# Tile 3's logits and ranks ahead of the first expert's row products, and one weight piece split on other engines

## The chip, the cores and the metric

The kernel runs on one core of a Trainium2 chip. A core has the matrix engine TensorE (PE; its weight loads are listed apart as PEld), VectorE (DVE), ScalarE (ACT), GpSimd (POOL) and SyncE (SP), and 16 DMA engines that they feed through queues. Each engine works through its own instructions in order and waits on semaphores for the others. The metric is the time of one launch in microseconds on the device; each time is one run or the median of several.

## The reference

Two layers, each a token mixer (attention, mLSTM and a state-space branch) followed by a mixture of experts, over 512 tokens of 1024 features. What the change touches lies between the output projection and the first experts:

```python
mix = jnp.einsum('bsc,cd->bsd', heads, w_out[l])
x = _layernorm(DEEPNORM_ALPHA * x + mix, ln1_g[l], ln1_b[l])
...
glog = jnp.einsum('bsd,dg->bsg', x, wg) + bg                 # 4 groups
gp, gi = lax.top_k(jax.nn.softmax(glog, -1), 1)              # the best group
elog = jnp.einsum('bsd,gde->bsge', x, we) + be               # 4 experts in each
elog = jnp.einsum('bsge,bsg->bse', elog, one_hot(gi[..., 0]))
ep, ei = lax.top_k(jax.nn.softmax(elog, -1), 2)              # the best two of it
ep = ep / jnp.sum(ep, -1, keepdims=True)
combine = jnp.sum(one_hot(gi * 4 + ei, 16) * (gp * ep)[..., None], axis=2)
h = jax.nn.silu(einsum(x, w_gate)) * einsum(x, w_up)         # for each of 16 experts
h = h * combine[..., None]
return jnp.einsum('bsef,efd->bsd', h, w_down)
```

So each token goes to two of 16 experts. The kernel computes an expert only for the tokens that chose it, in blocks of 96 rows.

## The kernel before

Tokens stand in four tiles of 128. Float32 products are made of three passes over operands that are split into a high part (a copy on ScalarE) and a low part (a subtraction, on VectorE unless another engine is named). One helper, `split`, does this; its line is L409. Most other instructions go through a second helper that records them, and so have line 229 whatever issued them. A weight piece is 128x1024; an expert has six: four for its two first products (up and gate) and two for the last (down).

The stage in question runs once in each layer, around 320 to 370 us in layer 0 and 530 us later in layer 1. For each tile it makes the second half of the output projection, adds it to the residual, normalizes it, and computes the 20 router logits of the tile from transposed rows. From the logits it ranks groups and experts with comparisons (`low` is a constant mask that breaks ties), which gives `al`, a tile's one-hot of chosen experts. Matmuls of `al` with a triangle of ones (`strict`) and with ones (`onesb`) count each token's place within its expert's block; `key` is that place, and `ohf` (expert 0) and `ohs` (the others) are one-hots of `key` against 0 to 95. Expert 0's rows are not gathered but made on TensorE, as products of each tile with `ohf`. Every other expert gets an index: matmuls of `ohs` with a table of row numbers, then VectorE's `slr` and `slx`. GpSimd then gathers the rows by that index from `x1d`, a copy of the normalized tiles in DRAM (L1445), TensorE transposes them and VectorE and ScalarE split them.

The order in which this stage is written out is the string `WSEQ`, one step a word, with a tile's number behind most letters. A framework then assigns instructions to engines by this order and by when it expects operands, so that neighbouring steps may change places on an engine.

- `S` splits a piece of expert 0; `A` issues weight loads for the coming experts as far as buffers are free (`ahead`, L276 in the queue).
- `m` is a tile's projection; `e` adds it to the residual, transposes the tile's half on TensorE and has ScalarE copy it out of PSUM; `b` and `r` are mean, variance and reciprocal root; `g` and `f` normalize, one half of the columns on ScalarE and GpSimd (L1791 and L1799), the other on VectorE, and `f` ends with the store to `x1d` (L1802); `k` stores the tile to `acc` as well (L1806).
- `l` multiplies the transposed tile with the router's weights `wrg`; `c` finishes its logits `lg`; `Kab` ranks tiles a to b-1 and makes their one-hots.
- `Z` is expert 0's row product of one tile; `H` makes expert 1's index and gathers its rows.

The transposed halves of two tiles share one buffer of the pool from which weight loads get theirs. Stores and loads alike stand in SyncE's queue, in the order of the text, so a load that waits for a buffer holds back the store behind it. Expert 0's first three pieces are split in `S0` to `S2`; the rest of those below `PX` right behind the stage, with GpSimd doing the subtraction, in buffers that the projection has given back:

```python
for n in range(PRE, PX):          # PRE = 3, PX = 4
    ex[0].split(n, G, True)
```

A piece that has not been split by then is split when its product is written out, by ScalarE and VectorE.

Of the kernel before, what the change touches and what calls it, by code (L numbers as in the profile page):

```python
# [61 lines left out]
RES3 = 8  # L62
PROG = 1
SPARE = 0
PX = 4
RES2 = 12
LP = 30
NPA = 3
# [15 lines left out]
HOLD = 8  # L84
HK = 0
HE = 0
WSEQ = 'S0 S1 S2 A m0 e0 b0 r0 r0 r0 r0 g0 A m1 e1 b1 r1 r1 r1 r1 g1 l0 c0 f0 k0 A m2 l1 c1 K02 e2 b2 r2 r2 r2 r2 g2 f1 k1 A m3 Z0 Z1 l2 c2 f2 k2 e3 b3 r3 r3 g3 r3 r3 f3 K23 Z2 l3 c3 K34 H Z3'
WPIN = ''
NU = 7
WOG = (0, 2)  # L90
# [121 lines left out]
def tile_trunk(ctx: ExitStack, tc: tile.TileContext, ins, out, dbg=None, depth=DEPTH):  # L212
# [22 lines left out]
    V, A, G, T = Pinned(nc.vector, "V"), Pinned(nc.scalar, "A"), nc.gpsimd, Pinned(nc.tensor, "T")  # L235
# [20 lines left out]
    def small(shape, dt=F32, tag="s", bufs=1):  # L256
        return sm.tile(shape, dt, name=nm(tag), tag=tag, bufs=bufs)
# [162 lines left out]
    def mm3(p, ah, al, bh, bl, start=True, stop=True):  # L420
        T.matmul(p, ah, bh, start=start, stop=False)
        T.matmul(p, ah, bl, start=False, stop=False)
        T.matmul(p, al, bh, start=False, stop=stop)
# [134 lines left out]
    for l in range(depth):  # L558
# [1054 lines left out]
        def ahead(keep, upto=6 * E):  # L1613

            while todo and len(pool.whole) > keep and pool.spare(SPARE if keep == RES0 else 3) and 6 * todo[0][0].e + todo[0][1] < upto:
                m, n = todo.pop(0)
                if n not in m.raw:
                    m.load(n)
# [8 lines left out]
        order = (3, 2, 0, 1)  # L1627
# [28 lines left out]
        def wo_mm(p, i, q, w, first, last):  # L1656
            s = slice(i * 128, (i + 1) * 128)
            for a in range(2):
                j = 2 * q + a
                cc = slice(a * 512, a * 512 + 512)  # L1660
                mm3(p.ap, xh[j][:, s], xl[j][:, s], w[0][:, cc], w[1][:, cc],
                    start=(first and a == 0), stop=(last and a == 1))
# [34 lines left out]
        wo = []  # L1697
# [5 lines left out]
        def lend(q):  # L1703
            pool.whole += [NS + 2 * q, NS + 2 * q + 1]
# [15 lines left out]
        def route(a, b):  # L1720

            n = b - a
            ranks(a, b)


            dv = df.rearrange("p (i g) e -> p i g e", i=NT)
            V.tensor_tensor(oa[:, a:b], dv[:, a:b, 1:5], thr4[:, None, None, 1].to_broadcast([128, n, 4, 4]), op=OP.is_lt)
            V.tensor_tensor(oh1[:, a:b].rearrange("p i g e -> p (i g) e"), df[:, a * 5:b * 5],
                            thr4[:, None, 0].to_broadcast([128, n * 5, 4]), op=OP.is_lt)
            V.tensor_tensor(al[:, a:b].rearrange("p i (g e) -> p i g e", g=4), oa[:, a:b], bc(oh1[:, a:b, 0]), op=OP.mult)  # L1730
            if not prk:
                prk.append(P5.get(NT * E))
            p = prk[0]
            v = p.v("p (i e) -> p i e", i=NT)
            if a == 0:
                T.matmul(p[:, 0:b * E], strict, al[:, 0:b].rearrange("p i e -> p (i e)"), start=True, stop=False,
                         skip_group_check=True)
            for i in range(a):
                T.matmul(v[:, a:b], onesb, al[:, i, None, :].to_broadcast([128, n, E]), start=(i == 0), stop=False,
                         skip_group_check=True)  # L1740
            for i in range(a, b - 1):
                T.matmul(v[:, i + 1:b], onesb, al[:, i, None, :].to_broadcast([128, b - 1 - i, E]),
                         start=False, stop=False, skip_group_check=True)
            if a:
                T.matmul(p[:, a * E:b * E], strict, al[:, a:b].rearrange("p i e -> p (i e)"), start=False, stop=True,
                         skip_group_check=True)
            r = V.scalar_tensor_tensor(key[:, a:b], v[:, a:b], 1.0, al[:, a:b], op0=OP.add, op1=OP.mult)
            for e in range(2):
                ex[e].hot(key[:, :, e], a, b)
            return r  # L1750

        class Tile_:
# [1 line left out]
                self.i, self.z, self.s = i, xr[i], slice(i * 128, (i + 1) * 128)  # L1754
                self.ph = PHS[i]

            def mm(self):
                p = self.p = ps[self.i] if PROG else P4.get()
                for a, q in list(enumerate(order))[PROG:]:
                    wo_mm(p, self.i, q, wo[a], a == 0, a == 3)  # L1760

            def evac(self):
                self.ev = evac(self.p, self.i, 1)
# [46 lines left out]
        def mark():  # L1810
            return tc.keep_in_program_order(G.memset(small([128, 1], tag="mark", bufs=2), 0.0))

        tiles = [Tile_(i) for i in range(NT)]
        kins, mk = None, []
        for c in WSEQ.split():
            if c[0] == "Z":
                i = int(c[1])
                ex[0].xz(i, tiles[i].z)
                if i < NT - 1:
                    tiles[i].z.free()  # L1820
                continue
            if c[0] == "K":
                pin[0] = WPIN
                kins = route(int(c[1]), int(c[2]))
                pin[0] = False
                continue
            if c == "H":
                ex[1].go()
                mk += [None, mark()]
                continue  # L1830
            if c == "A":
                ahead(RES0)
                continue
            if c[0] == "S":
                pin[0] = WPIN
                ex[0].split(int(c[1]), lent=True)
                pin[0] = False
                continue
            t = tiles[int(c[1])]
            pin[0] = WPIN  # L1840
            {"m": t.mm, "e": t.evac, "b": t.bn, "r": t.r, "l": t.logits, "c": t.lgs, "g": t.g, "f": t.f, "k": t.keep}[c[0]]()
            pin[0] = False
        free(*wo[PROG:])
        free(lgt, prk, ln1)
# [1 line left out]
        for q in order[PROG:]:  # L1846
            lend(q)
        for n in range(PRE, PX):
            ex[0].split(n, G, True)
# [4 lines left out]
        for _ in range(NU):  # L1854
            m, n = todo.pop(0)
# [10 lines left out]
        m1, m2 = small([128, NT, 5], tag="m1"), small([128, NT, 4], tag="m2")  # L1866
# [116 lines left out]
        with tc.If(rv > 0), tc.For_i(0, rv, 1):  # L1983
# [43 lines left out]
            m = Expert(load_gu, load_dn)  # L2027
# [120 lines left out]
        for i in range(NT):  # L2148
            n = norms[i]
# [79 lines left out]
```

## Time and profile before

| | |
|---|---|
| median of 3 runs | 1076.05 us (1075.78 to 1082.33) |
| profiled execution | 1076.42 us, of which the span is 1074.7 us |
| mean granted clock of TensorE | 0.971 of full |
| busy share of the span | TensorE 93%, VectorE 78%, ScalarE 60%, GpSimd 25% |

The profile is one execution. Times below are us from the start of its span. A group's last bracket on a timeline tells for how long the engine had stood idle and which operation, of which engine, ended that. A granted clock of 1.00 is TensorE's full 2.4 GHz, 0.50 its 1.2 GHz.

### The profile page before, as it was taken

How to read it: one execution, taken by the hardware profiler on the slowest of the kernel's cores; microseconds unless marked ns; L12 is line 12 of the kernel's file. 1: busy time of each engine (PE TensorE's matmuls, PEld its weight loads, DVE VectorE, ACT ScalarE, POOL GpSimd, SP SyncE). 2: the span in 40 equal slices, each digit the busy share in tenths (PEclk: the TensorE clock that was granted, in tenths of full speed). 3: DMA queues.
4: the chain of work that ended last, by engine and by line, in shares of the span. 5: the costliest groups of instructions: out<-in, count | busy, mean ns of one | idle time of the engine just before them, and what ended most of it. 6: DMA issues, size and time to landing. Idle time of an engine off the chain costs nothing. (4 is left out here: it accounts for less than half of the span.)

```text
span 1074.7 us, 15552 instructions
## 1 busy us (share of the span) xinstructions
PE 999.9 (93%) x5310; PEld 741.5 (69%) x5310; DVE 834.5 (78%) x1830; ACT 645.0 (60%) x1182; POOL 273.7 (25%) x234
## 2 busy tenths in 40 slices
PE   6999999979998899999999999989799979999995
PEld 6876787546688666666698768866467866666653
DVE  8995558787648699999969946577875677999996
ACT  5565546646423588888645564566463327878874
POOL 1000002322004155566000000023210322655652
PEclk9999999999997899999999999999899988999998
DMA  7211100133646789995632120012347477999833
GB/s 303 69 51 39 40 21 26 54 118 129 233 157 236 265 280 346 339 340 179 212 125 70 40 68 1 21 40 62 115 156 268 147 275 223 310 341 344 299 80 155
DMA packets 51795, 176.76 MB, mean 164 GB/s; under 512 B 8169, under 2 KB 8681, under 8 KB 51712
## 3 DMA queue, kind: packets, MB, share of 16 engines
q1 hardware_dynamic: 45216, 160.42, 41.9%
q0 software_dynamic: 6496, 15.31, 6.1%
q8 instruction: 42, 0.69, 0.3%
q14 instruction: 41, 0.34, 0.1%
HBM read 159.61 MB, written 23.59 MB: 170 GB/s over the span
## 5 line engine op out<-in xcount | busy, mean ns | idle before, releaser
L229 PE MATMUL b<-s,s 128*128 128x512 f32 (+9 forms) x1262 | 318.9, 404 | 15.5 <-DVE s L229 8.2
L229 PE MATMUL b<-xt,s 128*128 128x512 f32 (+3 forms) x1354 | 295.2, 363 | 12.4 <-ACT s L229 8.8
L229 DVE TENSOR_TENSOR s<-s,s 128x1024 fp32r<-128x1024 f32 (+5 forms) x256 | 250.5, 1004 | 50.1 <-ACT s L229 41.6
L229 ACT ACTIVATE s<-s 128x1024 fp32r<-128x1024 f32 (+6 forms) x242 | 213.4, 924 | 85.0 <-DVE s L229 31.7
L229 PEld LDWEIGHTS b<-xt,s 128*128 128x128 f32 (+2 forms) x1354 | 213.6, 185 | 70.4 <-issue 11.3
L229 PE MATMUL b<-s,xt 128*128 128x256 f32 (+2 forms) x1096 | 255.3, 365 | 0.4 <-POOL s L1522 0.4
L229 PEld LDWEIGHTS b<-s,s 128*128 128x128 f32 (+3 forms) x1262 | 177.2, 173 | 98.3 <-DVE s L229 25.8
L229 ACT ACTIVATE s<-b 128x512 f32<-128x512 f32 (+7 forms) x266 | 128.4, 497 | 173.4 <-PE b L229 164.9
L229 PEld LDWEIGHTS b<-s,xt 128*128 128x128 f32 (+1 forms) x1096 | 172.1, 184 | 44.4 <-issue 4.8
L229 PE MATMUL b<-ident,s 128*128 128x128 f32 (+3 forms) x736 | 109.2, 277 | 25.5 <-DMA s<-x1d,slx 8.8
L229 PEld LDWEIGHTS b<-ident,s 128*128 128x128 f32 (+3 forms) x736 | 82.7, 155 | 59.7 <-ACT s L229 13.9
L229 ACT ACTIVATE xt<-s 128x1024 fp32r<-128x1024 f32 (+1 forms) x84 | 86.3, 1036 | 23.8 <-PE b L229 14.5
L229 DVE TENSOR_TENSOR xt<-s,xt 128x512 fp32r<-128x512 f32 (+1 forms) x76 | 79.7, 1053 | 14.2 <-ACT xt L229 14.0
L1597 POOL DMA_INDIRECT acc<-s,slx x28 | 53.1, 1896 | 103.1 <-ACT s L229 100.6
L229 ACT ACTIVATE s<-b,mx,qsc 128x512 f32<-128x512 f32 x64 | 49.8, 784 | 25.4 <-DVE mx L229 25.1
L1337 POOL TENSOR_SCALAR s<-s,sums 128x512 f32<-128x512 f32 x48 | 37.6, 790 | 105.1 <-DVE sums L229 93.0
L1445 POOL DMA_INDIRECT s<-x1d,slx x30 | 44.3, 1477 | 64.6 <-PE b L229 28.2
L229 PE MATMUL b<-xt 128*96 128x512 f32 x184 | 58.3, 402 | 0.0
L1093 POOL MEMSET s<- 128x780 f32 x4 | 3.0, 755 | 215.7 <-DVE s L229 182.0
L229 DVE TENSOR_REDUCE mx<-b 128x1 f32<-128x512 f32 x64 | 43.2, 686 | 17.4 <-PE b L229 17.1
L229 ACT ACTIVATE xt<-b 128x384 fp32r<-128x384 f32 (+1 forms) x72 | 33.8, 518 | 36.7 <-PE b L229 36.5
L229 ACT ACTIVATE s<-b,slw 96x512 f32<-96x512 f32 (+1 forms) x60 | 39.1, 682 | 18.3 <-PE b L229 12.5
(255 smaller groups left out, 1056.6 us busy)
## 6 DMA issues: line engine op xcount, KB each, us to landing
s<-in_w_gu_dram SPq DMA_DIRECT2D x128, 512.0 KB, 8.3
s<-in_expert_w_down_dram SPq DMA_DIRECT2D x64, 512.0 KB, 8.2
s<-in_w_inp_dram SPq DMA_DIRECT2D x36, 512.0 KB, 4.5
s<-in_w_outp_dram SPq DMA_DIRECT2D x16, 512.0 KB, 4.4
x1d<-s SPq DMA_DIRECT2D x8, 512.0 KB, 2.9
acc<-s SPq DMA_DIRECT2D x8, 512.0 KB, 4.0
s<-acc SPq DMA_DIRECT2D x8, 512.0 KB, 6.9
s<-in_x_t_dram SPq DMA_DIRECT2D x4, 512.0 KB, 5.4
```

Of the source, the lines that this page charges most:

```text
L229: r = f(*a, **kw)
L1093: G.memset(cb.ap, 0.0)
L1337: (V if hd in NORMV else G).tensor_scalar(P.ap, P.ap, sums, 0.0, op0=OP.mult, op1=OP.add)
L1445: self.ga = G.indirect_dma_start(out=self.xg[:BLK], out_offset=None, in_=x1d[0:128 * n, :], in_offset=bass.IndirectOffsetOnAxis(ap=ix[:BLK ...
L1597: G.indirect_dma_start(out=acc[:, :], out_offset=bass.IndirectOffsetOnAxis(ap=self.ix[:BLK, 0:1], axis=0), in_=yt[:BLK], in_offset=None, b ...
```

## The change

Three edits. `PX` becomes 3, so no piece of expert 0 is split on GpSimd any more, and the fourth is split when it is used. `WSEQ` is written in another order behind the second tile's steps. And a tile's projection can be written in two parts: `n3` is parts 1 and 2 of tile 3, `o3` part 3. The logits of tile 2 and the ranks of tile 2 now stand between the two; the residual sum of tile 3 stands behind the ranks of tile 2 and expert 0's row product of tile 0; and tile 3's logits and ranks stand ahead of the row products of tiles 1 and 2.

```diff
-PX = 4
+PX = 3
...
-WSEQ = 'S0 S1 S2 A m0 e0 b0 r0 r0 r0 r0 g0 A m1 e1 b1 r1 r1 r1 r1 g1 l0 c0 f0 k0 A m2 l1 c1 K02 e2 b2 r2 r2 r2 r2 g2 f1 k1 A m3 Z0 Z1 l2 c2 f2 k2 e3 b3 r3 r3 g3 r3 r3 f3 K23 Z2 l3 c3 K34 H Z3'
+WSEQ = ('S0 S1 S2 A m0 e0 b0 r0 r0 r0 r0 g0 A m1 e1 b1 r1 r1 r1 r1 g1 l0 c0 f0 k0 A m2 l1 c1 K02 e2 b2 r2 r2 r2 r2 g2 f1 k1 '
+        'A n3 l2 c2 K23 Z0 o3 e3 b3 r3 r3 g3 r3 r3 l3 c3 f2 k2 K34 Z1 Z2 f3 H Z3')
...
-            def mm(self):
+            def mm(self, parts=range(PROG, 4)):
                 p = self.p = ps[self.i] if PROG else P4.get()
-                for a, q in list(enumerate(order))[PROG:]:
-                    wo_mm(p, self.i, q, wo[a], a == 0, a == 3)
+                for a in parts:
+                    wo_mm(p, self.i, order[a], wo[a], a == 0, a == 3)
...
-            {"m": t.mm, "e": t.evac, "b": t.bn, "r": t.r, "l": t.logits, "c": t.lgs, "g": t.g, "f": t.f, "k": t.keep}[c[0]]()
+            {"m": t.mm, "n": lambda: t.mm(range(PROG, 3)), "o": lambda: t.mm((3,)), "e": t.evac, "b": t.bn, "r": t.r, "l": t.logits, "c": t.lgs, "g": t.g, "f": t.f, "k": t.keep}[c[0]]()
```

What becomes of this on the engines, in layer 0; layer 1 has the same order around it.

TensorE, from tile 2's logits (`b_75`) to tile 3's (`b_74`). `s_271` and `s_272` are tiles 0 and 1, `s_274` is tile 3, whose transposes go to `b_76`; `s_280` holds the transposed tiles, and `b_69` and `b_70` collect expert 0's rows. Before:

```order
L229 MATMUL b_75<-wrg_794,s_280_2541 128x20 x4
L229 LDWEIGHTS strict
L229 MATMUL b_73<-al_2764,strict 128x32
...
L229 MATMUL b_76<-ident,s_274_2532 128x128 x4
...
L229 MATMUL b_69<-ohf_2940,s_271_2526 128x96 x4
L229 MATMUL b_70<-ohf_2940,s_271_2526 128x96 x4
L229 MATMUL b_69<-ohf_2940,s_272_2528 128x96 x4
L229 MATMUL b_70<-ohf_2940,s_272_2528 128x96 x4
L229 MATMUL b_74<-wrg_794,s_280_2541 128x20 x4
```

And now:

```order
L230 MATMUL b_75<-wrg_794,s_280_2541 128x20 x4
...
L230 MATMUL b_72<-s_305_2722,xt 128x512
L230 LDWEIGHTS strict
L230 MATMUL b_73<-al_2764,strict 128x32
...
L230 MATMUL b_69<-ohf_2940,s_271_2526 128x96 x4
L230 MATMUL b_70<-ohf_2940,s_271_2526 128x96 x4
L230 MATMUL b_76<-ident,s_274_2532 128x128 x4
L230 MATMUL b_69<-ohf_2940,s_272_2528 128x96 x4
L230 MATMUL b_74<-wrg_794,s_280_2541 128x20 x4
L230 MATMUL b_70<-ohf_2940,s_272_2528 128x96 x4
```

Tile 2's logits moved ahead of the last five matmuls of tile 3's projection, tile 3's transposes behind the products of tile 0, and its logits ahead of the last four products of tile 1; the ranks of tile 2 stay behind both tiles' products.

VectorE at the same place: `b_72` is tile 3's sum in PSUM. Before:

```order
L229 SCALAR_TENSOR_TENSOR s_274_2532<-b_72,s_274_2532 128x512
L229 SCALAR_TENSOR_TENSOR key_2765<-b_73,al_2764 128x32
L229 SCALAR_TENSOR_TENSOR lg_2538<-wsb_795,nmean_2953,lg_2538 128x20
L229 TENSOR_TENSOR ohf_2940<-iota_128,key_2765 128x192
L229 TENSOR_TENSOR ohs_2942<-iota_128,key_2765 128x192
L229 SCALAR_TENSOR_TENSOR lg_2538<-lg_2538,nr_2957,wsb_795 128x20
```

And now:

```order
L230 SCALAR_TENSOR_TENSOR key_2765<-b_73,al_2764 128x32
L230 SCALAR_TENSOR_TENSOR lg_2538<-wsb_795,nmean_2953,lg_2538 128x20
L230 TENSOR_TENSOR ohf_2940<-iota_128,key_2765 128x192
L230 TENSOR_TENSOR ohs_2942<-iota_128,key_2765 128x192
L230 SCALAR_TENSOR_TENSOR lg_2538<-lg_2538,nr_2957,wsb_795 128x20
L230 SCALAR_TENSOR_TENSOR s_274_2532<-b_72,s_274_2532 128x512
```

The residual sum of tile 3 moved from ahead of key and one-hots of tiles 0 and 1 to behind them.

VectorE at the index of expert 1 (`slx_3097`) and the split of expert 0's rows (`s_365`). Before:

```order
L229 SCALAR_TENSOR_TENSOR slx_3097<-slr_3098,b_75 96x1
L229 TENSOR_REDUCE md_3164<-m_3152 128x4
L229 SCALAR_TENSOR_TENSOR more_3188<-b_74,more_3188 128x16
L229 TENSOR_TENSOR xt<-s_315_2776,xt 128x1024
L229 TENSOR_TENSOR s_365_3116<-b_69,s_364_3115 128x384
L229 TENSOR_TENSOR s_365_3116<-b_70,s_364_3115 128x384
L229 COPY slr_3127<-b_76 96x1
```

And now:

```order
L230 SCALAR_TENSOR_TENSOR slx_3097<-slr_3098,b_75 96x1
L230 SCALAR_TENSOR_TENSOR more_3186<-b_74,more_3186 128x16
L230 TENSOR_TENSOR xt<-s_296_2668,xt 128x1024
L230 COPY slr_3127<-b_76 96x1
L230 SCALAR_TENSOR_TENSOR more_3186<-b_74,more_3186 128x16
L230 TENSOR_TENSOR s_365_3116<-b_69,s_364_3115 128x384
L230 TENSOR_TENSOR s_365_3116<-b_70,s_364_3115 128x384
```

Where a subtraction for a piece of expert 1 (`s_315`) stood ahead of the split of expert 0's rows, there now stands the one for expert 0's fourth piece (`s_296`), and `s_315`'s comes behind it. The row of `s_296` on GpSimd, ahead of tile 2's additions, is gone. Further on, the index of expert 2 moved on VectorE from behind the two splits of expert 1's rows to ahead of them, and on TensorE the eight matmuls that sum the weights of experts 0 and 1 (`tokw`) from ahead of expert 1's transposes to behind them. On SyncE the read of `nblk`, the number of further blocks, stands among the weight loads in layer 0, 53 rows earlier.

## Rows read from the trace of the kernel before

**Rows 1.** The page, the busy time of each engine over the whole span: us, share of the span, and number of instructions behind the x.

```profile
PE 999.9 (93%) x5310; PEld 741.5 (69%) x5310; DVE 834.5 (78%) x1830; ACT 645.0 (60%) x1182; POOL 273.7 (25%) x234
```

**Rows 2.** The timeline of TensorE at the end of the routing: start in us from the span's start, us that the row's instructions took, engine, line, operation, written tile <- read tiles, shape, count; in square brackets the idle time just ahead and what ended it. The row at 861.91 is the one of layer 1 that answers to 331.93.

```profile
329.27 0.96 PE L229 MATMUL b<-wrg,s 128*128 128x20 f32 x8
331.93 0.18 PE L229 MATMUL b<-al,strict 128*128 128x32 bf16 x1 [1.70 <-DVE al L229]
...
332.62 1.13 PE L229 MATMUL b<-ident,s 128*128 128x128 f32 x4 [0.49 <-DVE s L229]
...
333.63 6.47 PE L229 MATMUL b<-ohf,s 128*128 128x96 f32 x32
339.94 0.99 PE L229 MATMUL b<-wrg,s 128*128 128x20 f32 x8
...
345.67 0.71 PE L229 MATMUL b<-ohf,s 128*128 128x96 f32 x2 [0.65 <-DVE ohf L229]
...
861.91 0.19 PE L229 MATMUL b<-al,strict 128*128 128x32 bf16 x1 [1.93 <-DVE al L229]
```

**Rows 3.** The timelines of GpSimd (POOL) and VectorE (DVE) over the same stretch, columns as in rows 2; the last row is of layer 1.

```profile
326.76 2.64 POOL L409 TENSOR_TENSOR xt<-s,xt 128x1024 fp32r<-128x1024 f32 x1 [1.01 <-ACT xt L229]
...
327.07 2.52 DVE L229 TENSOR_TENSOR s<-s,low 128x160 f32<-128x160 f32 x1
...
331.88 0.68 DVE L229 SCALAR_TENSOR_TENSOR s<-b,s 128x512 f32<-128x512 f32 x1
...
334.57 0.23 DVE L229 TENSOR_TENSOR s<-s,low 128x80 f32<-128x80 f32 x1
...
338.02 1.28 POOL L1799 TENSOR_TENSOR s<-s,s 128x512 f32<-128x512 f32 x1 [1.05 <-ACT s L229]
...
341.86 0.23 DVE L229 SCALAR_TENSOR_TENSOR lg<-lg,nr,wsb 128x20 f32<-128x20 f32 x1
...
343.90 0.18 DVE L229 TENSOR_TENSOR al<-oa,oh 128x16 bf16<-128x16 f32 x1
...
873.04 0.17 DVE L229 TENSOR_TENSOR al<-oa,oh 128x16 bf16<-128x16 f32 x1
```

**Rows 4.** Stretches of the span, one a row: from:to in us, its length, then the busy us (and instructions) of PE, PEld, DVE, ACT and POOL, the granted clock of TensorE, the busy share of the 16 DMA engines, and GB/s.

```profile
342.80:352.50 9.70, 9.05 (x42) 8.09 (x41) 6.96 (x37) 1.81 (x5) 1.45 (x2) 0.50 1.00 333
868.20:882.40 14.20, 13.20 (x101) 10.90 (x100) 10.76 (x57) 4.72 (x8) 2.25 (x3) 1.00 0.76 271
886.00:892.10 6.10, 5.99 (x26) 4.64 (x27) 3.33 (x8) 4.54 (x6) 1.36 (x1) 0.50 0.45 165
895.80:899.00 3.20, 3.20 (x13) 2.60 (x14) 1.60 (x4) 2.15 (x4) 0.00 (x0) 0.50 0.89 315
```

**Rows 5.** The issue of transfers. First SyncE's queue (SPq): one weight load and the store of tile 3's rows to `x1d` in layer 0, and that store in layer 1. Then the DMA table, whose last number is the us from issue to landing: the store at 341.43, and the store of tile 2 at 333.09. Then the two gathers of expert 1's rows on GpSimd's timeline, layer 0 and 1, and their landing in the DMA table, in the same order.

```profile
341.00 0.33 SPq L276 DMA_DIRECT2D s<-in_w_gu_dram  x1
341.43 0.37 SPq L1802 DMA_DIRECT2D x1d<-s  x1
...
871.02 0.36 SPq L1802 DMA_DIRECT2D x1d<-s  x1
...
x1d<-s SPq DMA_DIRECT2D x1, 512.0 KB, 5.4
x1d<-s SPq DMA_DIRECT2D x1, 512.0 KB, 2.7
...
347.83 1.34 POOL L1445 DMA_INDIRECT s<-x1d,slx  x1 [8.53 <-PE b L229]
...
877.02 1.05 POOL L1445 DMA_INDIRECT s<-x1d,slx  x1 [7.74 <-DMA s<-in_expert_w_down_dram]
...
s<-x1d,slx POOLq DMA_INDIRECT x1, 8.4
s<-x1d,slx POOLq DMA_INDIRECT x1, 9.0
```

**Rows 6.** The timelines of VectorE and of TensorE at experts 0, 1 and 2, columns as in rows 2. `slx` is an expert's row index as VectorE writes it (expert 1's at 346.67, expert 2's at 359.12 and, in layer 1, at 888.94); the subtraction at 346.89 is half of the split of one weight piece; `ident,s 96*128` are the transposes of an expert's gathered rows (expert 1's at 357.09 and 886.11, expert 2's at 365.39 and 895.76); `tokw,ohs` sums weights behind expert 0's first products.

```profile
346.67 0.14 DVE L229 SCALAR_TENSOR_TENSOR slx<-slr,b 96x1 int32<-96x1 f32 x1
346.89 1.21 DVE L229 TENSOR_TENSOR xt<-s,xt 128x1024 fp32r<-128x1024 f32 x1
...
359.12 0.14 DVE L229 SCALAR_TENSOR_TENSOR slx<-slr,b 96x1 int32<-96x1 f32 x1
...
888.94 0.14 DVE L229 SCALAR_TENSOR_TENSOR slx<-slr,b 96x1 int32<-96x1 f32 x1
...
357.09 0.86 PE L229 MATMUL b<-ident,s 96*128 96x96 f32 x8
...
365.39 0.88 PE L229 MATMUL b<-ident,s 96*128 96x96 f32 x8 [2.68 <-DMA s<-x1d,slx]
...
874.08 0.43 PE L229 MATMUL b<-ohf,s 128*128 128x96 f32 x2 [0.62 <-DVE ohf L229]
...
881.92 0.48 PE L229 MATMUL b<-tokw,ohs 128*96 128x3 bf16 x8
...
886.11 1.54 PE L229 MATMUL b<-ident,s 96*128 96x96 f32 x8 [3.71 <-DMA s<-x1d,slx]
...
895.76 1.54 PE L229 MATMUL b<-ident,s 96*128 96x96 f32 x8 [2.43 <-DMA s<-x1d,slx]
```

**Rows 7.** The waits between 366 and 500 us, in the expert loop of layer 0: engine, tile and line that waited <- what it waited for, us in total, times, and the longest.

```profile
DVE slr L229 <- PE b L229: 5.8, 12, 1.0
```

## The prediction

> **What bounds the kernel now.** I read the page first: TensorE is busy 93% of the span [rows 1], so time can only come from the places where it waits or runs at its lower clock. The change touches one stage of each layer, the end of the output projection, the routing and the start of the expert loop, so next I read TensorE's timeline there. In layer 0 it is without a gap until 330.2, waits 1.70 us for `al` (the one-hot of the chosen experts of tiles 0 and 1), then runs transposes, the row products of tiles 0 and 1, tile 3's logits, and tile 3's row products from 345.67 [rows 2]. Layer 1 is the same, 529.98 us later. The timelines of VectorE and GpSimd say why `al` is late [rows 3]. SyncE's and GpSimd's say how the stage goes on: tile 3's rows must be stored to `x1d`, then GpSimd gathers expert 1's rows [rows 5], and TensorE turns those and, behind them, computes the index of expert 2, whose gather it then waits for: 2.68 us in layer 0, 2.43 us in layer 1, and in layer 1 another 3.71 us for expert 1's [rows 6]. So at the end of this stage two gathers, one behind the other, are the chain. From there on the expert loop is a steady pace in which VectorE and TensorE wait for each other by tenths [rows 7] and for no weights; what the first gathers gain moves everything after it.
>
> **The split leaves GpSimd.** The subtraction for expert 0's fourth piece ran on GpSimd from 326.76 for 2.64 us. VectorE's multiply by `low`, 128x160, started at 327.07 and took 2.52 us; the same operation on half the elements took 0.23 us [rows 3]. So some 2.52 - 0.46 = 2.06 us of VectorE were a stall beside GpSimd. Without it `al`, whose first reader started at 331.93, comes at 331.93 - 2.06 = 329.9, before TensorE is done at 330.2 [rows 2, 3]: the wait of 1.70 us goes. The same piece now costs ScalarE a copy and VectorE a subtraction later: one of that size took 1.21 us [rows 6]. ScalarE has room. VectorE's stands right behind expert 1's index and ahead of the split of expert 0's rows, which holds the first expert's products back by some 0.6 us (from 0, if TensorE is late itself, to 1.21).
>
> **The order around tile 3.** The row products of tile 0 no longer stand behind tile 3's transposes (332.62 to 333.63 [rows 2]); with `al` earlier they start at about 331.6, not 333.63, since GpSimd's next addition (1.28 us [rows 3]) still stands beside the one-hots. But tile 3's sum from PSUM, at 331.88 before [rows 3], now stands behind key and one-hots and comes at 331.9 again, and its transposes wait for tile 0's products, half of the 6.47 us of [rows 2]: 1.6 us at the full clock to 3.2 us at half. So the transposes start at 333.2 to 334.8, against 332.62, and GpSimd's last addition on tile 3, which ended at 339.30, ends at 339.9 to 341.5. Here the change loses. What it gains is the logits: their last read (340.93 [rows 2]) frees a buffer that a weight load at 341.00 waits for, and the store of tile 3 stands behind that load, at 341.43 and 871.02 [rows 5], that is 341.04 in layer 0's count. With the logits some 4 us earlier the store waits only for the addition: 339.9 to 341.6, and I take 340.3, 1.1 and 0.7 us earlier. It took 5.4 us to land with the load just ahead of it, tile 2's alone 2.7 us [rows 5]; the load is now gone by then but two others follow, so I take 4.0: landed at 344.3.
>
> **Tile 3's ranks.** VectorE reaches them behind GpSimd's last addition, at 340.1, because a two-input operation stands still beside it as above. From the logits' last step at 341.86 to `al` took 2.2 us [rows 3], so `al` comes at 342.3, not 344.06, and tile 3's products start 0.9 us later, as in layer 1 (873.2 to 874.08): 343.2, against 345.67 and 344.1. TensorE, done with tile 2's products by then, waits about 2 us ahead of them. The index of expert 1 follows 1.1 us behind the products' start (345.67 to 346.81 [rows 2, 6]): 344.3. The gather began 0.9 to 1.0 us after the later of store and index (346.83 to 347.83 [rows 5]), now 345.2: 2.6 us earlier than 347.83, 1.8 us earlier than 877.02. It landed 8.4 and 9.0 us later [rows 5]; with the same loads ahead of it I keep that: 353.6 and, in layer 1, 884.2.
>
> A page's rule speaks against this place. The moved subtraction runs just when the gather is issued; before, one of 1.21 us from 346.89 ended at 348.10 and the gather had begun at 347.83 [rows 5, 6], so it was not held. The Trainium skill, SBUF — State Buffer, section SBUF: two separate sides, says that VectorE, with two SBUF inputs, and a GpSimd instruction that reads SBUF lock each other out for a whole instruction. By that rule each gather could come up to 1.2 us later, and the sum below would be 2.4 us smaller; the row says no, and I leave it out of the sum.
>
> **Where the first expert ends.** From tile 3's first product to the end of expert 0's first products layer 1 took 7.84 us at the full clock (874.08 to 881.92 [rows 4, 6]). Now: 343.2 + 7.8 + 0.6 = 351.6, ahead of the gather. A stretch at half clock, as from 342.8 to 352.5 [rows 4], costs half its length and brings it to 355 or 355.5. So the transposes of expert 1 start at 353.6 to 355.5 in layer 0, against 357.09: I take 354.4, 2.7 us earlier. In layer 1, at 884.2 to 885.5, against 886.11: 884.4, 1.7 us earlier.
>
> **From there to the second gather.** The weight products of experts 0 and 1, 8 small matmuls, now stand behind the transposes instead of ahead (0.35 to 0.6 us), but the index stands ahead of the two splits of 0.5 us each. Before, from transposes to index: 2.17 us in layer 0 and 2.97 us in layer 1, there at half clock [rows 4, 6]. Now between 1.5 and 2.6: I take a gain of 0.1 and 0.2 us. What pays for it is expert 1's first products, whose split comes some 2 us later; the wait for the second gather (2.68 and 2.43 us [rows 6]) covers that, with about 0.4 us to spare in each layer. If that cover goes, it costs up to 0.5 us each.
>
> **Sum.** 2.7 + 1.7 + 0.1 + 0.2 = 4.7 us. The profiled execution took 1076.42 us, of which 1074.7 us are the span, 0.4 us over the median of 1076.05: 1076.05 - 4.7 = 1071.4. The load of `nblk` on SyncE, now among the weight loads, is hidden: no engine waits for weights there.
>
> **Rivals.** *The clock holds.* If the shorter waits leave TensorE at full clock through expert 0, and the low stretch behind the second gather (895.8 to 899.0 [rows 4]) goes too, layer 0 gains 3.5 and layer 1 2 us, and 1.6 us each for the stretch: 8.7, so 1067.4. Against it: a 2 us wait remains in front of tile 3's products. *The store moves the other way.* The wait for `al` goes, but with tile 0's products at half clock the addition ends at 341.5, so the store takes the logits' place as the last: issued at 341.6 it is as late as before, and TensorE only waits longer ahead of tile 3's ranks. What is left is the emptier queue, about 1 us in layer 0 and 0.5 us in layer 1: 1074.5. The order speaks for it in part: tile 2's ranks still stand behind the products of tiles 0 and 1, so the change does less than it says. *Slower.* The new wait ahead of tile 3's products drops the clock, and it stays at half through all of expert 0. Then 2 x 7.8 + 0.6 = 16.2 us from 343.2 end at 359.4 and 889.4, against 357.09 and 886.11: 2.3 + 3.3 = 5.6 us, so 1081.6. It decides from a low stretch of some 9.6 us on; the longest one here is 9.7 us [rows 4], and layer 1 had none in that place.
>
> **How the numbers follow.** Forecast, 1069.5 to 1073.5: 0.53. Clock holds: 0.15. Store: 0.20. Slower: 0.10. Something else: 0.02. The range 1067.5 to 1076.0 takes in the forecast, the store and half of the first rival. About 1% is what a measurement of this kernel can tell from no change; 10.8 us is out of reach of every case but the unnamed, so within 1% has 0.95, faster 0.03, slower 0.02.
>
> **What would show it.** GpSimd's 128x1024 subtraction in the projection's end is gone and the multiply by `low` takes 0.3 us; TensorE has no gap ahead of the first ranks but one of 1 us behind them and about 2 us ahead of tile 3's; the store of tile 3 is issued before 341.4 and 871.0, the gather of expert 1 by 2 to 3 us earlier; the first subtraction of the piece stands at the gather's issue; the steady pace keeps its 10.2 us. The prediction is wrong if the gather of expert 1 takes longer to land, or if expert 1's products outlast the second gather.

## The result and the profile after

The changed kernel took 1068.95 us (median of 4 runs, 1067.59 to 1070.35), against 1071.4 forecast and a range of 1067.5 to 1076.0. The ratio to the kernel before is 0.9915, 95% interval 0.9888 to 0.9943; two more sets beside the kernel before gave 0.9894 and 0.9901. So it is faster by about 1%, 9 to 11 us. The sign was right and the time lies in the range, but the sum of 4.7 us is half of the gain, and that the time lies in the range is in part luck: the forecast was counted from 1076.05 us, which lies low among the runs of the kernel before (medians of 1077.5 to 1079.6 in the three later sets). By the measured ratios 1076.05 would become 1064.6 to 1066.9, below the range.

In the profiled execution the span fell from 1074.7 to 1067.8 us, by 6.9. The two changed stages gained more, 12.7 (below), and places that the change doesn't touch took the difference back. The largest, 2.6 us, is around 136 us, in layer 0's mixer: this execution ran at half clock there, that of before (second fence) didn't. Some 2 us more went between the two stages, around 660 us, where both executions fell and this one for longer (granted clock 0.72 from 658 to 670, before 0.86). Rows are stretches, the third figure from the end is the granted clock.

```profile
136.00:138.00 2.00, 2.00 (x10) 1.90 (x10) 0.64 (x5) 0.00 (x0) 0.00 (x0) 0.50 0.00 0
```

```profile
136.00:138.00 2.00, 2.00 (x18) 1.96 (x18) 1.60 (x13) 0.71 (x3) 0.00 (x0) 1.00 0.00 0
```

Of the 14 executions profiled for this study, six have that low stretch, three of them of kernels with `PX = 4` and three with `PX = 3`; of the three of the changed kernel itself one has it. It comes and goes by itself, and so whole spans of one execution each say little here; the stages have to be compared by themselves.

TensorE after the change, the stage of layer 0, and from 858.34 that of layer 1 (columns as in rows 2):

```profile
331.59 1.65 PE L230 MATMUL b<-s,xt 128*128 128x512 f32 x6
333.09 0.19 PE L230 MATMUL b<-al,strict 128*128 128x32 bf16 x1
...
334.68 2.00 PE L230 MATMUL b<-ohf,s 128*128 128x96 f32 x16 [0.91 <-DVE ohf L230]
336.52 0.65 PE L230 MATMUL b<-ident,s 128*128 128x128 f32 x4
...
337.92 1.07 PE L230 MATMUL b<-wrg,s 128*128 128x20 f32 x8
...
344.94 0.17 PE L230 MATMUL b<-al,strict 128*128 128x16 bf16 x1 [2.22 <-DVE al L230]
...
345.76 0.43 PE L230 MATMUL b<-ohf,s 128*128 128x96 f32 x2 [0.63 <-DVE ohf L230]
...
356.68 0.82 PE L230 MATMUL b<-ident,s 96*128 96x96 f32 x8
...
360.30 2.02 PE L230 MATMUL b<-xt 128*96 128x512 f32 x4 [1.37 <-DVE xt L230]
...
364.25 1.03 PE L230 MATMUL b<-ident,s 96*128 96x96 f32 x10
...
373.90 1.02 PE L230 MATMUL b<-ident,s 96*128 96x96 f32 x10
...
858.34 1.65 PE L230 MATMUL b<-s,xt 128*128 128x512 f32 x6
...
882.91 0.82 PE L230 MATMUL b<-ident,s 96*128 96x96 f32 x8
...
889.81 0.88 PE L230 MATMUL b<-ident,s 96*128 96x96 f32 x8 [0.36 <-DMA s<-x1d,slx]
...
899.03 1.02 PE L230 MATMUL b<-ident,s 96*128 96x96 f32 x10
```

Against [rows 2]: the projection and tile 2's logits, in either order, end at 333.24 (before, at 330.23; the 3.0 us come from ahead of the stage), and there is no gap in front of the first ranks. The row products of tile 0 start 1.4 us behind that end, before 3.4, and run at full clock. Against [rows 6]: expert 1's transposes no longer wait for their gather in layer 1, and the second gather costs 0.36 us in layer 1 and nothing in layer 0, where it cost 2.43 and 2.68.

Granted clock after the change: the products of tiles 0 to 2, then the stretch behind the wait of 2.22 us, and its like in layer 1:

```profile
333.30:340.00 6.70, 5.51 (x50) 5.40 (x50) 6.20 (x23) 1.30 (x3) 2.19 (x2) 1.00 0.70 276
346.35:353.10 6.75, 6.75 (x27) 5.32 (x26) 5.16 (x22) 2.71 (x5) 1.39 (x2) 0.50 0.97 336
...
872.00:878.20 6.20, 6.07 (x26) 5.47 (x27) 4.64 (x21) 2.54 (x5) 1.47 (x2) 0.50 0.94 314
```

The low stretches behind the second gather, as in the last row of [rows 4], are gone, but one stands behind the wait for `xt` in layer 0 (360 to 363.4).

The two sums on which the rest is read: T1, from the end of tile 3's projection and tile 2's logits (whichever comes last) to expert 1's transposes, and T2, from there to expert 3's. Two rows of layer 1 before:

```profile
859.01 0.96 PE L229 MATMUL b<-wrg,s 128*128 128x20 f32 x8
...
906.47 1.02 PE L229 MATMUL b<-ident,s 96*128 96x96 f32 x10
```

Before, T1 was 357.09 - 330.23 = 26.9 us and 886.11 - 859.97 = 26.1 (layer 0 and 1, rows 2 and 6), T2 376.1 - 357.1 = 19.0 and 906.5 - 886.1 = 20.4. After, 23.4 and 22.9, and 17.2 and 16.1. That is 6.6 us from T1 and 6.0 from T2. Of T2's 6.0 some 3.5 came by expert 2's transposes (365.39 - 357.09 = 8.3 us and 9.7 before, 7.6 and 6.9 after), the rest behind them, where the low clock went.

### The profile page after: what moved, and what is told of

Read it like the earlier page. It is cut to its first block, busy times and chain, and to the rows that moved or that the text cites. A ratio compares the mean times of both kernels' runs of the same rounds, so it can differ in the third digit from the quotient of the medians.

```text
span 1067.8 us, 15553 instructions
## 1 busy us (share of the span) xinstructions
PE 996.5 (93%) x5310; PEld 739.2 (69%) x5310; DVE 836.0 (78%) x1832; ACT 644.6 (60%) x1182; POOL 267.2 (25%) x232
## 5 line engine op out<-in xcount | busy, mean ns | idle before, releaser
L230 PE MATMUL b<-xt,s 128*128 128x512 f32 (+3 forms) x1484 | 327.1, 367 | 13.8 <-ACT s L230 8.6
L230 PE MATMUL b<-s,s 128*128 128x512 f32 (+7 forms) x1308 | 324.7, 404 | 14.0 <-ACT s L230 7.1
L230 DVE TENSOR_TENSOR s<-s,s 128x1024 fp32r<-128x1024 f32 (+8 forms) x254 | 247.6, 1000 | 50.5 <-ACT s L230 41.7
L230 PEld LDWEIGHTS b<-s,s 128*128 128x128 f32 (+3 forms) x1308 | 185.0, 173 | 99.7 <-DVE s L230 22.6
L230 ACT ACTIVATE s<-b 128x512 f32<-128x512 f32 (+8 forms) x282 | 135.0, 496 | 191.2 <-PE b L230 182.3
L230 ACT ACTIVATE s<-s 128x1024 fp32r<-128x1024 f32 (+5 forms) x219 | 191.6, 910 | 85.1 <-DVE s L230 31.8
L230 PE MATMUL b<-s,xt 128*128 128x256 f32 (+2 forms) x944 | 209.1, 362 | 0.4 <-POOL s L1523 0.4
L230 PEld LDWEIGHTS b<-s,xt 128*128 128x128 f32 (+1 forms) x944 | 150.6, 192 | 34.7 <-issue 4.8
L230 DVE TENSOR_TENSOR xt<-s,xt 128x1024 fp32r<-128x1024 f32 (+1 forms) x106 | 118.3, 1122 | 13.8 <-ACT xt L230 13.7
L230 ACT ACTIVATE xt<-s 128x1024 fp32r<-128x1024 f32 (+1 forms) x107 | 110.4, 1042 | 26.1 <-PE b L230 17.7
L230 DVE TENSOR_REDUCE mx<-b 128x1 f32<-128x512 f32 x64 | 43.2, 686 | 18.3 <-PE b L230 17.9
L230 DVE TENSOR_TENSOR s<-b,s 128x192 fp32r<-128x192 f32 (+3 forms) x92 | 46.9, 524 | 4.6 <-POOL s L1127 2.6
```

The source lines that it names most:

```text
L230: r = f(*a, **kw)
```

## The experiments

Twelve runs, each against the kernel before on the same chip. The table gives the ratio with its interval, and T1 and T2 of each profile, read as above (us, layer 0 / layer 1; in bfill2 and bfillw T1 starts ahead of the added work).

| kernel | ratio | T1 | T2 | T1 + T2 against before |
|---|---|---|---|---|
| before | 1 | 26.9 / 26.1 | 19.0 / 20.4 | |
| after (again) | 0.9894 [0.9859, 0.9929] | 23.5 / 23.0 | 16.1 / 17.3 | -12.6 |
| after (again2) | 0.9901 [0.9872, 0.9931] | 23.2 / 22.5 | 16.0 / 17.4 | -13.3 |
| px3 | 0.9870 [0.9834, 0.9906] | 22.8 / 21.5 | 17.2 / 18.0 | -12.9 |
| px3b | 0.9882 [0.9852, 0.9911] | 22.8 / 22.5 | 15.9 / 16.4 | -14.8 |
| order4 | 1.0015 [0.9995, 1.0035] | 27.6 / 26.8 | 19.5 / 19.2 | +0.7 |
| pooldummy | 0.9926 [0.9902, 0.9950] | 26.7 / 22.6 | 17.3 / 18.2 | -7.6 |
| bfill2 | 0.9991 [0.9971, 1.0011] | 27.1 / 25.3 | 19.7 / 18.3 | -2.0 |
| bfillw | 0.9958 [0.9936, 0.9979] | 21.8 / 27.0 | 20.4 / 19.3 | -3.9 |
| gfirst | 0.9947 [0.9920, 0.9974] | 27.1 / 24.9 | 19.3 / 17.3 | -3.8 |
| fill | 0.9921 [0.9892, 0.9951] | 23.1 / 24.7 | 18.3 / 17.8 | -8.5 |
| px3h6 | 0.9921 [0.9893, 0.9950] | 22.8 / 22.7 | 19.0 / 22.1 | -5.8 |
| px3phs | 0.9916 [0.9888, 0.9943] | 24.0 / 24.7 | 16.1 / 17.3 | -10.2 |

A ratio of 0.99 is 10.8 us, so T1 + T2 of a single profile follows the measured ratios to within 4 us. The order is the same but for neighbours that lie within 3 us of each other.

**Which edit?** px3 and px3b are edit 1 alone, order4 the other two, again and again2 the changed kernel.

```diff
# px3, px3b: the kernel before with
-PX = 4
+PX = 3
# order4: the changed kernel with
-PX = 3
+PX = 4
```

> Edit 1 alone: the fourth piece is not split on GpSimd, the old order of the stage stays. Theory A (the stall on VectorE is the main cause, and TensorE's clock the way in which it costs): al comes some 2 us earlier, the wait of 1.70 us ahead of the first ranks shrinks below 0.4, TensorE stays at the full clock through the products of tiles 0 and 1 (6.5 us become 4), tile 3's logits are read some 4 us earlier, the gather of expert 1 starts 2.5 to 3.5 us earlier against the end of the projection, and the time is 6 to 10 us shorter than before, ratio 0.991 to 0.995. Theory B (the order does it: logits and ranks ahead of the products): the wait goes but tile 3's chain stays where it is behind the products, the gather gains 1 us at most, ratio 0.997 to 1.000.

> Edits 2 and 3 alone: the new order, with the fourth piece still split on GpSimd. Theory A: the subtraction on GpSimd stalls the multiply by low as before (2 to 2.5 us for one of 0.3), TensorE waits 1.5 to 2.2 us for al and falls to half clock behind it, so little is gained: ratio 0.996 to 1.000. Theory B: the order brings the logits and the store forward in any case: ratio 0.991 to 0.995.

> The changed kernel once more, on the same chip as the three others, as their yardstick: ratio 0.989 to 0.994, as measured. In its profile the stretch from 134 to 142 us, at half clock in the first profile of the changed kernel and not in that of before, lies ahead of the changed stage: if it comes and goes by itself, it is at full clock here or in one of the others.

> Edit 1 alone once more, beside the changed kernel on the same chip. Theory A, as borne out so far: edit 1 carries the whole gain and the new order nothing or a little less than nothing, so the two stand within 0.3% of each other, this one at 0.986 to 0.991 of before.

> The changed kernel, third time, for that comparison: ratio to before 0.988 to 0.992. If the order carried a share of the gain, it would stand at least 0.3% under edit 1 alone.

Edit 1 alone gives all of the gain, 0.9870 and 0.9882, more than theory A had at first expected; the new order alone gives none, 1.0015. With edit 1 in place, the order adds nothing either: 0.9894 and 0.9901 beside them, a little more, inside the intervals. In px3 the old order stands, and tile 3's logits still come early, since the products ahead of them run at full clock:

```profile
331.13 3.79 PE L229 MATMUL b<-ohf,s 128*128 128x96 f32 x32
334.76 0.99 PE L229 MATMUL b<-wrg,s 128*128 128x20 f32 x8
```

Counted from the projection's end, px3's logits start 5.1 us behind it (334.76 - 329.62), the changed kernel's 4.7 (337.92 - 333.24), those before 9.7 [rows 2]. In order4 GpSimd's subtraction is back, and with it the stall, the gaps and the low clock (VectorE, then TensorE):

```profile
329.66 2.50 DVE L230 TENSOR_TENSOR s<-s,low 128x160 f32<-128x160 f32 x1
```

```profile
333.98 0.18 PE L230 MATMUL b<-al,strict 128*128 128x32 bf16 x1 [1.06 <-DVE al L230]
...
336.16 3.70 PE L230 MATMUL b<-ohf,s 128*128 128x96 f32 x16 [1.22 <-DVE ohf L230]
```

The products of tile 0 with `ohf` took 3.70 us there and 2.00 in the changed kernel. Theory A held on which edit it is.

**Is it the stall?** pooldummy is px3 with the old copy and subtraction put back beside it, for nobody.

```diff
+h, lo = Q.get(1024, last=True, full=True), Q.get(1024, last=True, full=True)
+split(h.ap, lo.ap, ex[0].raw[3].ap, G)
+free(h, lo)
```

> Edit 1 alone (the fourth piece is split where it is used, by ScalarE and VectorE), plus the copy and the subtraction on GpSimd that the kernel before had in that place, now into buffers that nobody reads. Theory A (edit 1 gains because GpSimd no longer stalls VectorE): the multiply by low takes 2.5 us again, TensorE waits for al again, and the whole gain is lost: ratio to before 0.997 to 1.003. Theory E (the gain is in where the fourth piece is split, or in what its buffers release): most of the gain stays, ratio 0.987 to 0.992.

The stall and the wait came back in both layers, but 0.9926 lies between the two theories: theory A alone is refuted. T2 stayed short, 17.3 and 18.2. T1 was long in layer 0 and, with the same wait, short in layer 1, where the clock did not fall:

```profile
335.27 0.18 PE L229 MATMUL b<-al,strict 128*128 128x32 bf16 x1 [1.69 <-DVE al L229]
...
336.85 6.82 PE L229 MATMUL b<-ohf,s 128*128 128x96 f32 x32
...
865.95 0.18 PE L229 MATMUL b<-al,strict 128*128 128x32 bf16 x1 [1.74 <-DVE al L229]
...
867.55 3.78 PE L229 MATMUL b<-ohf,s 128*128 128x96 f32 x32
```

So edit 1 has two effects: the stall, which bears on T1, and something else, which sets T2.

**T1: late `al`, or the clock behind the wait?** bfill2 and bfillw are the kernel before with TensorE kept at work while it waits: 16 narrow instructions in the one, 6 wide ones in the other, which are placed ahead of the first ranks.

```diff
# bfill2, behind tile 2's logits
+for _ in range(2):
+    d = P5.get(20)
+    for k in range(4):
+        T.matmul(d.ap, t[:, k * 128:(k + 1) * 128], wrg[:, 4 * hf + k, :], start=(k == 0), stop=(k == 3))
...
# bfillw, in the same place
+d = P5.get()
+for k in range(6):
+    T.matmul(d.ap, xh[2 * order[3]][:, 384:512], wo[3][0][:, 0:512], start=k == 0, stop=k == 5)
...
```

> The kernel before, with tile 2's eight-instruction logits product repeated twice into a PSUM tile that nobody reads, 2 x 0.96 us of TensorE work in the place of its wait of 1.70 us for al. Nothing else moves. al comes as late as before. Theory C (the wait costs through the clock that falls behind it): TensorE shows the full clock from 332 to 339 us and from 862 to 868, the products of tiles 0 and 1 take 4 us instead of 6.5, and the time falls by 3 to 8 us, ratio 0.9925 to 0.997. Theory D (what counts is that al is late, whatever TensorE does meanwhile): the same time as before to within 1 us, ratio 0.999 to 1.001.

> The kernel before, with six wide matmuls (512 columns, into a PSUM tile that nobody reads) behind tile 2's logits and ahead of the first ranks: about 1.5 us of work in TensorE's wait of 1.70 us for al, of the kind that it does in the projection. al comes as late as before. Theory C (the wait costs through the clock that falls behind it): the granted clock is 1.00 through the products of tiles 0 and 1, which take about 4 us instead of 6.5, tile 3's logits come 2 to 3 us earlier, and the time falls by 4 to 8 us, ratio 0.993 to 0.997. Theory D (what counts is that al is late): the same as before, ratio 0.998 to 1.002. If the clock falls all the same, the wait was not what dropped it.

bfill2 gained nothing, as theory D had it, but it did not test what it was meant to: TensorE hardly waited, and its clock fell all the same (0.61 on average from 335.3 to 344).

```profile
332.76 2.53 PE L229 MATMUL b<-wrg,s 128*128 128x20 f32 x22
335.46 0.18 PE L229 MATMUL b<-al,strict 128*128 128x32 bf16 x1 [0.17 <-DVE al L229]
...
337.05 6.82 PE L229 MATMUL b<-ohf,s 128*128 128x96 f32 x32
```

bfillw did. In layer 0 the clock stayed at 1.00, and in layer 1 it fell from 864 on:

```profile
331.44 0.18 PE L229 MATMUL b<-al,strict 128*128 128x32 bf16 x1 [0.25 <-DVE al L229]
...
333.88 3.78 PE L229 MATMUL b<-ohf,s 128*128 128x96 f32 x32 [0.31 <-DVE ohf L229]
...
863.50 5.41 PE L229 MATMUL b<-ohf,s 128*128 128x96 f32 x32 [0.31 <-DVE ohf L229]
```

With `al` as late as before, T1 was 21.8 us where the clock held, no longer than with edit 1, and 27.0 where it fell. pooldummy shows the same pair, 22.6 and 26.7; where the clock held in its layer 1 as in px3's, it is 1.0 us longer than px3's 21.5. So the 1.7 us by which `al` is late cost about 1 us by themselves; what cost 4 us or more was the clock behind them. Theory C held, where the fill kept the clock. These are pairs of single layers, but all profiles point the same way: without the stall (the eight profiles of kernels with `PX = 3` other than pooldummy) the products of tiles 0 and 1 ran at full clock in all 16 layers; with it and no fill (before, order4, gfirst, pooldummy) they ran below it in seven layers of eight.

**T2: the second gather.** Where the profile has its landing, and apart from gfirst and px3h6 below, the second gather landed 5.1 to 5.8 us after its issue in the kernels with `PX = 4`, and 3.9 to 4.6 with `PX = 3`. For the first profile of the changed kernel there is only an upper bound: in layer 1 it was issued at 885.75 and TensorE stopped waiting for it at 889.81. The busy share of the DMA engines (last figure but one) behind its issue at 360.06 before, and at 359.52 after:

```profile
360.00:362.00 2.00, 1.35 (x6) 0.64 (x4) 1.53 (x3) 1.99 (x3) 1.52 (x1) 1.00 0.01 4
362.00:364.00 2.00, 0.57 (x6) 0.38 (x6) 1.53 (x6) 1.37 (x3) 0.37 (x1) 1.00 0.70 189
364.00:366.00 2.00, 0.61 (x7) 0.62 (x8) 1.46 (x3) 0.05 (x2) 0.90 (x1) 1.00 1.04 371
```

```profile
359.50:361.50 2.00, 1.21 (x3) 0.91 (x4) 2.00 (x5) 0.00 (x0) 1.10 (x1) 0.61 0.35 84
361.50:363.50 2.00, 2.00 (x6) 1.26 (x6) 0.00 (x1) 0.00 (x0) 0.00 (x0) 0.53 0.20 76
```

SyncE's queue in the same place, before and after; the last two of these four loads for expert 5 went out from 361.4 us before, while the gather was under way, and from 364.1 after:

```profile
354.16 8.07 SPq L276 DMA_DIRECT2D s<-in_w_gu_dram  x4
```

```profile
354.10 10.75 SPq L277 DMA_DIRECT2D s<-in_w_gu_dram  x4
```

They waited for TensorE, for buffers that it gives back with expert 1's first products. gfirst holds these two and the two behind them in the kernel before until the gather has landed, and moves no instruction of the engines that compute.

```diff
+h, held[0] = held[0], ex[2].ga if m.e == 5 and n > 1 else held[0]
 m.load(n)
+held[0] = h
```

> The kernel before, with the four weight loads of expert 5 that go out 2 us after expert 2's gather held back until that gather has landed; no instruction changes its place. Theory H (in the kernel before those loads slow the second gather, which lands 5.3 to 5.9 us after its issue against 4.0 to 4.2 where no load runs beside it): it lands 1.2 to 1.8 us sooner, TensorE's wait ahead of expert 2's transposes falls from 2.7 to about 1.5 us, and the time falls by 2 to 4 us, ratio 0.996 to 0.998. Theory I (the landing is the gather's own): the same landing and the same time, ratio 0.999 to 1.001, or slower by the later weights.

The gather landed in 4.4 and 4.3 us, TensorE's wait for it fell to 1.79 and 1.39 us from 2.68 and 2.43 [rows 6], and the ratio is 0.9947. Theory H held; the gain is a little above what was expected of it, which lies within its interval. Its profile shows the gain of T2 in layer 1 alone (17.3 us for 20.4): in layer 0 the wait became shorter but the clock still fell behind it, and T2 stayed at 19.3. So the loads are shown to slow the gather; how much of T2's 6.0 us is theirs alone is not.

```profile
367.70 1.54 PE L229 MATMUL b<-ident,s 96*128 96x96 f32 x8 [1.79 <-DMA s<-x1d,slx]
...
898.89 0.88 PE L229 MATMUL b<-ident,s 96*128 96x96 f32 x8 [1.39 <-DMA s<-x1d,slx]
```

px3h6 tried the same on the first gather, with edit 1.

```diff
-HOLD = 8
+HOLD = 6
```

> Edit 1 alone, with the weight loads that follow expert 1's gather held back until it has landed, not until it has been issued. If those loads are what makes the first gather land 8.4 to 9 us after its issue, it lands in 5 to 7 us, layer 1's wait of 3.1 us ahead of expert 1's transposes goes, and the time is 1 to 4 us under edit 1 alone, ratio to before 0.983 to 0.987. If it is the loads already under way at its issue, the landing stays at 8 us or more and the later weights cost up to 2 us: ratio 0.987 to 0.990.

The first gather landed in 8.4 and 8.6 us all the same, so the loads issued behind it are not what makes it slow. That it is those already under way is likely (the DMA engines were 0.93 busy from 343.5 to 346 us, behind its issue at 343.56) but was not tested. The loads that were held came later and met the second gather instead, which took 5.3 and 7.5 us; TensorE waited for it:

```profile
360.67 0.88 PE L229 MATMUL b<-ident,s 96*128 96x96 f32 x8 [1.66 <-DMA s<-x1d,slx]
...
889.25 1.54 PE L229 MATMUL b<-ident,s 96*128 96x96 f32 x8 [3.88 <-DMA s<-x1d,slx]
```

At 0.9921 against px3b's 0.9882 beside it, it seems to have lost by this collision, which bears gfirst out from the other side; the two intervals overlap.

**What is late next.** fill makes tile 2's product twice, which keeps TensorE at work in the new wait ahead of tile 3's ranks; px3phs takes GpSimd out of tile 3's normalization.

```diff
# fill: the changed kernel, ahead of tile 2's product
+for k in range(KD):
+    T.matmul(p[:, (k % 4) * BLK:(k % 4 + 1) * BLK], tiles[i].z[:, k * 128:(k + 1) * 128],
+             ex[0].ohf[:, i], start=k % 4 == 0, stop=k > 3, skip_group_check=True)
...
# px3phs: px3 with
-PHS = (512, 512, 512, 512)
+PHS = (512, 512, 512, 0)
```

> The changed kernel, with tile 2's row product done a second time into a PSUM tile that nobody reads, 2.0 us of TensorE work in its wait of 2.2 us ahead of tile 3's ranks, behind which it fell to half clock for 6.8 us in both layers. Theory F (from there on the gather of expert 1 is the chain, with TensorE only just behind it): the clock stays up, expert 0 ends some 3 us earlier, and TensorE then waits for the gather, which lands 8.4 to 9 us after its issue: 0 to 1 us gained in each layer, ratio to before 0.987 to 0.991. Theory G (TensorE's clock is the chain up to the second gather): 3 us in each layer, ratio 0.982 to 0.985.

> Edit 1 alone, and tile 3 normalized on VectorE alone (both halves) instead of half of it on ScalarE and GpSimd. If GpSimd's two additions on tile 3 hold VectorE up (0.85 and 1.19 us for operations that take 0.17 and 0.31 alone), TensorE's wait of 0.97 us for key goes, VectorE pays 2 x 0.7 us for the wider halves, and the store of tile 3 needs no GpSimd: between 2 us faster and 1 us slower than edit 1 alone, ratio to before 0.985 to 0.989. If GpSimd's part were free for VectorE, the two wider halves would make it 1 to 3 us slower than edit 1 alone, ratio 0.988 to 0.991.

fill's ratio, 0.9921, shows no gain over the changed kernel's 0.9894 to 0.9915, let alone theory G's 3 us a layer. In layer 0 the clock held through expert 0, TensorE was done with expert 0's first products 2.7 us sooner, counted from the projection's end, and waited for the gather:

```profile
342.66 0.17 PE L230 MATMUL b<-al,strict 128*128 128x16 bf16 x1 [0.36 <-DVE al L230]
...
343.78 1.78 PE L230 MATMUL b<-ohf,s 128*128 128x96 f32 x14
...
354.05 0.85 PE L230 MATMUL b<-ident,s 96*128 96x96 f32 x8 [2.22 <-DMA s<-x1d,slx]
```

In layer 1 the clock fell within the repeated product, and T1 grew. Theory F holds for layer 0; layer 1 decides nothing. px3phs, 0.9916, is not faster than px3: it lies above both ranges expected of it, though its interval reaches into them. VectorE's wider halves put a wait of 1.41 us ahead of tile 2's ranks in both layers. No kernel tried is shown to beat the changed one; edit 1 alone stands level with it.

## Why the prediction was right, and where its sum was short

**The split leaves GpSimd: right.** The multiply by `low` takes 0.32 us, not 2.52, and `al` is there before TensorE needs it.

```profile
329.99 0.32 DVE L230 TENSOR_TENSOR s<-s,low 128x160 f32<-128x160 f32 x1
```

Beside GpSimd it took 2.50 us in order4 and 2.52 in pooldummy, until 0.2 us behind the end of the other instruction. That is what the Trainium skill, SBUF — State Buffer, section SBUF: two separate sides, says of two engines on one port pair, and the traces agree. That this edit alone is the gain, the prediction did not say: it put half of the reason on the new order.

**The order around tile 3: the times came, the cause did not.** The products started 2.0 us sooner against the projection's end (forecast 2.0), tile 3's transposes 0.9 later (forecast 0.6 to 2.2), the store of tile 3 1.7 and 1.5 us sooner (1.1 and 0.7). But px3 has the earlier products and logits without the new order, and there the store went out 2.2 us sooner still, and the gather 0.7 and 1.4 us. The logits came sooner because the products of tiles 0 and 1 ran at full clock, which the prediction only noticed as a spread of 1.6 to 3.2 us on half of them.

**Tile 3's ranks and the first gather: right.** The waits ahead of tile 3's products came, 2.22 + 0.63 us (about 2 were named), and the gather went out 3.2 and 2.9 us sooner (2.6 and 1.8):

```profile
347.61 1.28 POOL L1446 DMA_INDIRECT s<-x1d,slx  x1 [4.92 <-DMA s<-in_expert_w_down_dram]
...
874.15 1.37 POOL L1446 DMA_INDIRECT s<-x1d,slx  x1 [4.69 <-DMA s<-in_expert_w_down_dram]
```

The moved subtraction did not hold it. It stands from 346.61 to 347.82, the gather began within it, 1.0 us behind the index, as before; so the lock of the Trainium skill, SBUF — State Buffer, section SBUF: two separate sides, which the prediction applied to the gather, does not show at this place.

```profile
346.46 0.14 DVE L230 SCALAR_TENSOR_TENSOR slx<-slr,b 96x1 int32<-96x1 f32 x1
...
346.61 1.21 DVE L230 TENSOR_TENSOR xt<-s,xt 128x1024 fp32r<-128x1024 f32 x1
```

**Where the first expert ends: a little short.** The half-clock stretch behind the new wait came, 6.8 us long where the prediction had reckoned with up to 9.7, and expert 1's transposes started 3.4 and 3.2 us sooner where 2.7 and 1.7 were forecast. They follow TensorE's own work without a wait, so the gather no longer set them.

**From there to the second gather: the term that was mis-sized.** It was forecast at 0.1 + 0.2 us and measured some 3.5 up to expert 2's transposes; 2.5 more came behind them, up to expert 3's, where the sum has no term at all (together T2's 6.0). The prediction looked only at the index, and let "the wait for the second gather" cover all else, as if its landing were fixed. The landing was not: it fell from 5.3 and 5.8 us to about 4 (3.9 to 4.2 in the two repeats). The likely reason is that expert 1's first products, which the prediction itself had put later ("whose split comes some 2 us later"), also gave their buffers back later, so that the weight loads that used to run beside the gather now follow it; gfirst shows that these loads slow it, and no run moved the buffers alone. With the wait, the low clock behind it went in layer 1 (895.8 to 899.0 in [rows 4]); in layer 0 it moved to behind the wait for `xt`. Only "if expert 1's products outlast the second gather" was named as a danger; they do, in layer 0, and the time from expert 1's transposes to expert 2's is still 0.7 us shorter there.

**The rivals.** "The clock holds" was half true: it fell behind the 2 us wait as argued against it, but the stretch behind the second gather went, and its gain of 8.7 us is nearer to the measured 9 to 11 than the forecast's 4.7. "The store moves the other way" did not come; the index, not the store, released the gather: the store went out at 342.71, and in the repeats it landed 3.0 us later. "Slower" did not come either: the clock fell behind the new wait, but for 6.8 us, short of the 9.6 from which it would have cost time.

**The chances.** "Within 1%" was given 0.95, and 10.8 us were held out of reach. The first ratio, 0.9915, is within 1%, the repeats, 0.9894 and 0.9901, stand on either side of the line: the gain itself is about 1%, so this chance was too high for the same reason as the sum was too low.

The pace of the loop stayed at 10.2 us (424.10 - 413.92 between transposes).

## What to carry to other kernels

When a wait goes, look not only at its length but at the clock behind it: here a wait of 1.7 us cost about 1 us where the clock held, and 4 us more where it fell. When work moves behind a transfer, ask which buffers it gives back and what loads these set off: the latency of a small gather on the critical path depends on what runs beside it (4 us here, or 5 to 6). And of a change in several parts, run each part alone before its order of work is credited with the gain.

## What the runs showed of the hardware

- TensorE's clock fell in bfill2 although it worked without a gap of 0.3 us on matmuls of 20 columns from 332.76 on; behind six of 512 columns in the same place it stayed up in layer 0 of bfillw and fell in layer 1.
- The same wait does not always drop it: 1.69 us did in layer 0 of pooldummy, 1.74 us didn't in layer 1. The Trainium skill, TensorE: Matmul & The Clock Gate, Part 1, says that the moment at which the clock changes varies from run to run of one kernel. The trace agrees in so far as the stretch at 136 us stands in one of three profiles of the changed kernel.
- A gather of 96 rows of 4 KB landed in 3.9 to 4.6 us where it was the second one and loads were late or held, in 5.1 to 7.5 with weight loads beside it, and in 7.8 to 9.1 where it was the first one, with DMA engines that were already busy (at most 6.9 in layer 0 of bfillw).
